# Operand sums in tiles of their own, and one unit of the second output pair ahead of the first pair's last

## The chip, the cores and the metric

The kernel runs on one core of a Trainium2 chip. The metric is the device time of one execution in microseconds (us); the time of a kernel is the median of several executions.

## The reference, cut to what matters

The program computes two layers of a transformer trunk on 512 tokens of width 1024: a token mixer (differential attention in the first layer, gated linear attention in the second) beside a cross-attention, and then a gated MLP with a causal convolution of width 3. The change lies in the MLP:

```python
def conv_ffn(h, w_up, conv_w, conv_b, w_down):
    u = h @ w_up                       # 1024 -> 2 * 2816
    c = conv(u, conv_w) + conv_b       # depthwise, width 3, causal
    a, g = jnp.split(c, 2, axis=-1)
    return (jax.nn.silu(g) * a) @ w_down
...
h = rms_norm(x, ffn_norm[i])
x = x + conv_ffn(h, w_up[i], conv_w[i], conv_b[i], w_down[i])
```

All of it is float32.

## The kernel before, in words

**Layout.** Activations lie transposed: a tile holds 128 channels (partitions) by 512 tokens. Each float32 operand of a matmul is split into two parts, `hi` (a rounded copy, made by ScalarE) and `lo` (operand minus `hi`, made by VectorE), and a product is three matmuls: hi x hi, hi x lo, lo x hi. Weights come from HBM in blocks of 128 x 1024 through three `raw` tiles (loads on SyncE's queue, line 266) and are split into `whi` and `wlo` tiles, six of each (`WB`, lines 257 and 260, or 308 to 312).

**The MLP in parts.** `ffn` (from line 1168) runs once for each layer. The 2816 hidden channels are 11 units of 256 channels (`q`), taken in three parts of 4, 4 and 3 units (`HALVES`). A unit is four up products: for each of its two tiles of 128 channels (`n`) one product for `a` ("ua") and one for the gate ("ug"). Each product is scaled and convolved by `conv` (lines 1248 to 1252: VectorE, ScalarE, VectorE, VectorE) into a `cvo` tile; then come SiLU on ScalarE (line 1446) and the multiplication on VectorE (line 1448). So there are four convolutions in a unit, of which the third and the fourth belong to its second tile. Some "ua" products (`SEVEN`) are done by seven products on sums instead.

**The down projection by seven products.** At the end of a part, `down` (from line 1339) multiplies the hidden channels by the down weights and adds the result to the residual. It takes 2 x 2 blocks: two tiles of channels, two tiles of output channels, and two halves of the tokens, and uses seven block products instead of eight, with sums of the operands. `seven(c, m)` (line 1352) is one unit of that: output pair `c` (0 to 3), hidden unit `m`. It has seven steps of three matmuls, 21 in all, each 128 x 128 by 256 columns (line 1359). `own` is its first three steps, which need only split halves of the hidden tiles themselves, and `mixed` is its other four, which need the sums. The list `seq` (lines 1402 to 1404) gives the order of the units by hand. When a unit is the last that uses a weight block, `release` lets a next block be made. A pair's last unit is followed by `decode` (line 1367), which adds the four banks to the residual. The last part of the first layer does without the seven products.

**The sums of the hidden operands.** When both tiles of a unit are there, `mid_sums` (line 1298) calls `combine` (line 1281), four subtractions of 256 columns (line 1287). For the last unit of a part VectorE makes them, in two `cvo` tiles of 512 columns. For the others POOL makes them, in one `wsum` tile of 1024 columns, and their split into `hi` and `lo` (`parts_of`, lines 1278 and 1279) is put off: it is kept in `later` and issued by `behind` (line 1313) behind the third convolution that follows. `wsum` has two buffers. They also hold the sums of the weight blocks, which POOL makes (`block_sums`, line 285; cast and subtraction at lines 311 and 312), and the sums of token tiles (`token_sums`, line 1325). `cvo` has six buffers.

**What sets the order.** TensorE runs in the order in which the program is written. On VectorE, ScalarE and SyncE a planner of the framework sets the order at build time: by when its own estimates say that an instruction's inputs and buffers are ready, earlier written ones first. POOL's sums keep their written order. At run time every engine takes its instructions strictly in the order so set.

Of the kernel before, what the change touches and what calls it, by code (L numbers as in the profile page):

```python
# [11 lines left out]
F32 = mybir.dt.float32  # L12
# [9 lines left out]
S = 512  # L22
# [162 lines left out]
def trunk(ctx, tc, head_d, x_t, mem_t, wpack, cols_a_d, cols_d, conv_d, gate_d, rel_bias, diff_lambda, consts, onehot, out):  # L185
    nc = tc.nc
    mm = nc.tensor.matmul
    V, A, G = nc.vector, nc.scalar, nc.gpsimd
# [23 lines left out]
    def blk(b, w=128):  # L212
        return slice(w * b, w * b + w)
# [40 lines left out]
    at = [0]  # L254
# [70 lines left out]
    def sum_tile():  # L325
        return sum_pool[0].tile([128, WTILE], F32, name="wsum", bufs=2)
# [172 lines left out]
    E = mybir.EngineType  # L499
    load = nc.sync.dma_start  # L500
    with tc.tile_pool(name="ini", bufs=1) as ip, tc.manual_schedule(engines={E.Activation, E.DVE, E.Pool, E.SP}):
# [34 lines left out]
        parts, acc, split_w = [], [None], [None]  # L536
# [631 lines left out]
    def ffn(pool, l, acc):  # L1168
# [37 lines left out]
            refill()  # L1206

        def ctile():
            return pool.tile([128, S], F32, name="cvo", bufs=6)

        def up(i, n):
            p, = take(1)
# [34 lines left out]
        def conv(p, j):  # L1247
            V.tensor_mul(p, p, rB)
            c = ctile()
            first = A.activation(c, p, AF.Identity, scale=cv[l][:, 2, j:j + 1], bias=cv[l][:, 3, j:j + 1])  # L1250
            V.scalar_tensor_tensor(c[:, 1:], p[:, :S - 1], cv[l][:, 1, j:j + 1], c[:, 1:], op0=ALU.mult, op1=ALU.add)
            final = V.scalar_tensor_tensor(c[:, 2:], p[:, :S - 2], cv[l][:, 0, j:j + 1], c[:, 2:], op0=ALU.mult, op1=ALU.add)
            if later:
                convs[0] += 1
                if convs[0] == 3:
                    convs[0] = 0
                    behind(first, final)
            return c
# [19 lines left out]
            A.copy(hi, t)  # L1278
            V.tensor_sub(lo, t, hi.bitcast(F32))  # L1279

        def combine(b2, b1, bh, bl, fh, fl, E, parts):
            t = [ctile(), ctile()] if E is V else [sum_tile()]
            q = [blk(i, 256) for i in range(4)]
            at = lambda i: t[i // 2][:, q[i % 2]] if E is V else t[0][:, q[i]]
            for i, x, y in ((0, b1[:, right], b1[:, left]), (1, b2[:, right], at(0)), (2, b2[:, right], b1[:, right]),
                            (3, b2[:, left], at(1))):
                ins = E.tensor_sub(at(i), x, y)  # L1287
                if E is G:
                    tc.keep_in_program_order(ins)
            parts(t)  # L1290
            return q
# [6 lines left out]
        def mid_sums(c2, ops, E):  # L1298
            h, lo = (pool.tile([128, 2 * S], F32R, name="mid2", bufs=8) for _ in range(2))

            def parts(t):
                for i, x in enumerate(t):
                    c = blk(i, 2 * S // len(t))
                    if E is V:
                        parts_of(x, h[:, c], lo[:, c])
                    else:
                        later.append((x, h[:, c], lo[:, c]))
            q = combine(*c2, *ops, E, parts)
            return operands([h[:, c] for c in q], [lo[:, c] for c in q], *ops)

        later, convs = [], [0]
# [8 lines left out]
        def scaled(k):  # L1320
            t = ctile()
            A.activation(t, xT[k], AF.Copy, scale=c_ffn(l, k))
            return t

        def token_sums(ks):
            (bh, bl), (fh, fl) = (tokens[k] for k in ks)
            tiles = [split_tiles(pool, "vs", 12) for _ in range(2)]

            def parts(t):
                for i, (hi, lo) in enumerate(tiles):  # L1330
                    parts_of(t[0][:, blk(i, S)], hi, lo)
            combine(scaled(ks[0]), scaled(ks[1]), None, None, None, None, G, parts)
            h, lo = ([t[i][:, c] for t in tiles for c in (left, right)] for i in range(2))
            sums_of[ks] = operands(h, lo, bh, bl, fh[:, left], fl[:, left])

        place = [(2, left), (0, left), (0, right), (1, left), (1, right), (2, right), (3, left)]
        steps, close = (1, 2, 0, 5, 4, 6, 3), {2: 0, 5: 2, 6: 3, 3: 1}

        def down(base, nq, mids, pairs, last, acc2):
            first = used[0]  # L1340
            whole = [plan[first + c][0][0] == "dw" for c in range(4)]
            banks, seen = {}, [set() for _ in range(4)]

            def start(c):
                begin(("dw" if whole[c] else "dn", l, base, c))
                banks[c] = take(2 if whole[c] else 4)

            def emitted(c, m):
                if m == nq - 1 or m % 2:
                    release(first + c, 1 if whole[c] else 2, m == nq - 1)  # L1350

            def seven(c, m, some=steps):
                while len(made) <= first + c or len(made[first + c]) <= m:
                    refill()
                for i in some:
                    b, h = place[i]
                    (hi, lo), (bh, bl) = made[first + c][m][i], mids[m][i]
                    for t, (w, v) in enumerate(((hi, bh), (hi, bl), (lo, bh))):
                        mm(banks[c][b][:, h], w, v, start=b not in seen[c], stop=m == nq - 1 and t == 2 and i in close)  # L1359
                        seen[c].add(b)  # L1360
                if some[-1] != steps[-1]:
                    return
                emitted(c, m)
                if m == nq - 1:
                    decode(c)

            def decode(c):
                b, x1, x2, u, y = banks[c], xT[2 * c], xT[2 * c + 1], ctile(), ctile()[:, left]
                A.copy(u[:, left], b[2][:, left])
                V.tensor_add(x1, x1, b[0])  # L1370
                V.tensor_add(y, u[:, left], b[2][:, right])
                V.tensor_add(u[:, right], y, b[1][:, right])
                V.tensor_add(y, y, b[3][:, left])
                V.tensor_add(x2, x2, b[1])
                V.tensor_add(x1, x1, u)
                x2v = x2.rearrange("p (h c) -> p h c", h=2)
                V.tensor_add(x2v, x2v, y.unsqueeze(1).to_broadcast([128, 2, 256]))
                if last and l == 1:
                    for n in (2 * c, 2 * c + 1):
                        nc.sync.dma_start(out[n], xT[n])  # L1380

            def eight(c, n, m0, m1, total=nq):
                parts = whole_piece(first + c)
                product(banks[c][n], parts, n, pairs, range(2 * m0, 2 * m1), 2 * total)

            if all(whole):
                for c0 in (0, 2):
                    cs = (c0, c0 + 1)
                    for c in cs:
                        start(c)  # L1390
                        for n in range(2):
                            eight(c, n, 0, nq - 1)
                        emitted(c, 1)
                    for c in cs:
                        for n in range(2):
                            eight(c, n, nq - 1, nq)
                            update(2 * c + n, banks[c][n], lambda k: c_attn(1, k), acc2)
                            nc.sync.dma_start(xres[2 * c + n], xT[2 * c + n])
                        emitted(c, nq - 1)
                return  # L1400
            own, mixed = steps[:3], steps[3:]
            seq = [(0, m, steps) for m in range(nq - 1)] + [(1, 0, steps), (0, nq - 1, own), (1, 1, own), (0, nq - 1, mixed)]
            seq += [(1, 1, mixed)] + [(1, m, steps) for m in range(2, nq)]
            seq += [(c, m, steps) for c in ((2,) if whole[3] else (2, 3)) for m in range(nq)]
            for c, m, some in seq:
                if c not in banks:
                    start(c)
                seven(c, m, some)
            if whole[3]:
                start(3)  # L1410
                eight(3, 0, 0, nq)
                V.tensor_add(xT[6], xT[6], banks[3][0])
                nc.sync.dma_start(out[6], xT[6])
                eight(3, 1, 0, nq - 1, nq - 1)
                V.tensor_add(xT[7], xT[7], banks[3][1])
                for t, p, queue in zip((left, right), take(2), (nc.sync, nc.scalar)):
                    p = p[:, :S // 2]
                    parts = made[first + 3]
                    product(p, parts[-2:], 1, [(bh[:, t], bl[:, t]) for bh, bl in pairs[-2:]])
                    V.tensor_add(xT[7][:, t], xT[7][:, t], p)  # L1420
                    queue.dma_start(out[7, :, t], xT[7][:, t])

        base, acc2 = 0, None
        for part, nq in enumerate(HALVES):
            mids, pairs = [], []
            last = part == len(HALVES) - 1
            for q in range(base, base + nq):
                c2, ops, at, cs = [], [], {}, {}
# [11 lines left out]
                for n in range(2):  # L1440
# [13 lines left out]
                    else:  # L1454
                        m = mid_tile()
# [104 lines left out]
```

## Time and profile before

| what | us |
|---|---|
| median of 3 runs (1152.59 to 1152.91) | 1152.81 |
| the profiled execution | 1153.93 |
| its span, first to last instruction | 1152.0 |
| TensorE busy in the span | 1141.9 |
| VectorE busy | 931.4 |
| ScalarE busy | 616.4 |
| POOL busy | 270.1 |

The profile is of one execution. PE is TensorE's matmul queue, PEld its weight loads, DVE VectorE, ACT ScalarE, POOL GpSimd, SP SyncE. A row of a timeline has the start in us from the beginning of the span, the duration in us, the engine, the line of the kernel, the operation, the tiles written and read (`out<-in`), their shapes, a count of merged instructions, and in brackets how long the engine was idle before it and what ended that. Ends of matmuls are modelled by the profiler, so waits of TensorE are better taken from the starts of its matmuls. A row of the waits has total us, times and longest us. The rows of a tile or line have the shortest, middle and longest duration in ns.

### The profile page before, as it was taken

How to read it: one execution, taken by the hardware profiler on the slowest of the kernel's cores; microseconds unless marked ns; L12 is line 12 of the kernel's file. 1: busy time of each engine (PE TensorE's matmuls, PEld its weight loads, DVE VectorE, ACT ScalarE, POOL GpSimd, SP SyncE). 2: the span in 40 equal slices, each digit the busy share in tenths (PEclk: the TensorE clock that was granted, in tenths of full speed). 3: DMA queues.
4: the chain of work that ended last, by engine and by line, in shares of the span. 5: the costliest groups of instructions: out<-in, count | busy, mean ns of one | idle time of the engine just before them, and what ended most of it. 6: DMA issues, size and time to landing. Idle time of an engine off the chain costs nothing.

```text
span 1152.0 us, 17410 instructions
## 1 busy us (share of the span) xinstructions
PE 1141.9 (99%) x6527; PEld 993.4 (86%) x6527; DVE 931.4 (81%) x1531; ACT 616.4 (54%) x1080; POOL 270.1 (23%) x318
## 2 busy tenths in 40 slices
PE   9999999999999999999999999999999999999998
PEld 7888888888889888898888888988888989899888
DVE  7676778688889789999677637777898988999987
ACT  6676686556554454445457634535664434544552
POOL 0000000003364423740000000000245432476241
PEclk9999999999999999999999999999999999999999
DMA  8522242133314332344252220333232343224312
GB/s 286 175 82 87 78 142 74 57 109 92 110 56 146 93 92 73 93 128 126 71 176 73 94 97 16 92 126 126 73 92 74 95 126 104 89 76 137 105 51 101
DMA packets 39666, 117.86 MB, mean 102 GB/s; under 512 B 4768, under 2 KB 7257, under 8 KB 39583
## 3 DMA queue, kind: packets, MB, share of 16 engines
q1 hardware_dynamic: 39150, 116.37, 32.0%
q8 instruction: 51, 0.84, 0.3%
q10 hardware_dynamic: 432, 0.39, 0.1%
q14 instruction: 33, 0.26, 0.1%
HBM read 112.54 MB, written 4.21 MB: 101 GB/s over the span
## 4 chain that ended last, share of the span: by engine, by line
PE 80%; DVE 13%; ACT 4%; issue 2%; POOL 1%; ACTq 0%; POOLq 0%; DVEq 0%
PE ps_mm L385 6%; PE ps_mm L408 6%; PE ps_mm L407 6%; PE ps_mm L409 6%; PE ps_mm L387 6%; PE ps_mm L386 6%; PE ps_lg L1359 3%; PE ps_sm L408 3%; PE ps_sm L407 3%; PE ps_sm L409 3%; PE ps_mm L1359 3%; PE ps_tp L224 3%; PE ps_lg L1233 3%; PE ps_tp L1359 2%; PE ps_sm L1359 2%; DVE mid L1279 2%
## 5 line engine op out<-in xcount | busy, mean ns | idle before, releaser
L260 DVE TENSOR_TENSOR wlo<-raw,whi 128x1024 fp32r<-128x1024 f32 (+5 forms) x166 | 188.7, 1148 | 74.7 <-ACT whi L257 73.8
L257 ACT CAST whi<-raw 128x1024 fp32r<-128x1024 f32 (+5 forms) x166 | 157.9, 967 | 104.9 <-PE ps_mm L408 24.3
L385 PE MATMUL ps_mm<-whi,xsh 128*128 128x512 f32 (+2 forms) x328 | 126.3, 385 | 0.0
L387 PE MATMUL ps_mm<-whi,xsl 128*128 128x512 f32 (+2 forms) x328 | 123.0, 375 | 0.0
L386 PE MATMUL ps_mm<-wlo,xsh 128*128 128x512 f32 (+2 forms) x328 | 122.8, 374 | 0.0
L407 PE MATMUL ps_mm<-xsh,whi 128*128 128x512 f32 x310 | 121.8, 393 | 0.0
L408 PE MATMUL ps_mm<-xsl,whi 128*128 128x512 f32 x310 | 120.9, 390 | 0.0
L409 PE MATMUL ps_mm<-xsh,wlo 128*128 128x512 f32 x310 | 120.8, 390 | 0.0
L285 POOL TENSOR_TENSOR wsum<-raw 128x256 f32<-128x256 f32 (+1 forms) x108 | 87.8, 834 | 117.5 <-DMA raw<-in_wpack_dram 64.1
L1287 POOL TENSOR_TENSOR wsum<-cvo 128x256 f32<-128x256 f32 x40 | 33.9, 848 | 226.7 <-DVE cvo L1448 140.9
L407 PE MATMUL ps_sm<-xsh,whi 128*128 128x512 f32 x202 | 78.6, 389 | 0.0
L408 PE MATMUL ps_sm<-xsl,whi 128*128 128x512 f32 x202 | 78.6, 389 | 0.0
L409 PE MATMUL ps_sm<-xsh,wlo 128*128 128x512 f32 x202 | 78.6, 389 | 0.0
L312 DVE TENSOR_TENSOR wlo<-wsum,whi 128x1024 fp32r<-128x1024 f32 (+1 forms) x54 | 70.6, 1307 | 8.9 <-ACT whi L311 8.9
L311 ACT CAST whi<-wsum 128x1024 fp32r<-128x1024 f32 (+1 forms) x54 | 51.9, 962 | 39.8 <-POOL wsum L285 39.5
L385 PEld LDWEIGHTS ps_mm<-whi,xsh 128*128 128x128 f32 x328 | 61.7, 188 | 11.4 <-issue 1.0
L387 PEld LDWEIGHTS ps_mm<-whi,xsl 128*128 128x128 f32 x328 | 61.7, 188 | 11.3
L386 PEld LDWEIGHTS ps_mm<-wlo,xsh 128*128 128x128 f32 x328 | 61.8, 188 | 10.1
L409 PEld LDWEIGHTS ps_mm<-xsh,wlo 128*128 128x128 f32 x310 | 58.2, 188 | 12.1
L407 PEld LDWEIGHTS ps_mm<-xsh,whi 128*128 128x128 f32 x310 | 58.2, 188 | 11.9 <-issue 0.3
L408 PEld LDWEIGHTS ps_mm<-xsl,whi 128*128 128x128 f32 x310 | 58.3, 188 | 11.9 <-DVE xsl L366 0.4
L1263 POOL MEMSET xsh<- 128x128 f32 x2 | 0.4, 210 | 277.5 <-PE ps_sm L408 191.0
(428 smaller groups left out, 3144.9 us busy)
## 6 DMA issues: line engine op xcount, KB each, us to landing
raw<-in_wpack_dram SPq DMA_DIRECT2D x178, 512.0 KB, 3.6
xt<-in_x_t_dram SPq DMA_DIRECT2D x15, 256.0 KB, 5.2
raw<-in_wpack_dram SPq DMA_DIRECT2D x15, 256.0 KB, 2.8
raw<-in_wpack_dram SPq DMA_DIRECT2D x8, 384.0 KB, 3.3
xres<-xt SPq DMA_DIRECT2D x8, 256.0 KB, 3.4
xt<-xres SPq DMA_DIRECT2D x8, 256.0 KB, 5.7
out_dram<-xt SPq DMA_DIRECT2D x7, 256.0 KB, 2.0
bt<-bias_d SPq DMA_DIRECT2D x6, 256.0 KB, 4.3
```

The costliest lines, as they stand in the source:

```text
L257: ins = A.copy(hi[:, c], raw[:, c])
L260: V.tensor_sub(lo[:, c], raw[:, c], hi[:, c].bitcast(F32))
L285: tc.keep_in_program_order(getattr(G, "tensor_" + op)(o, x, y))
L311: A.copy(h1[:, m], wsum[:, m])
L312: V.tensor_sub(l1[:, m], wsum[:, m], h1[:, m].bitcast(F32))
L385: mm(p, sh[k][:, blk(b)], hi, start=k == 0, stop=False)
L386: mm(p, sh[k][:, blk(b)], lo, start=False, stop=False)
L387: mm(p, sl[k][:, blk(b)], hi, start=False, stop=k == KT - 1)
L407: mm(p, hi[:, blk(n)], bh, start=i == first, stop=False)
L408: mm(p, hi[:, blk(n)], bl, start=False, stop=False)
L409: mm(p, lo[:, blk(n)], bh, start=False, stop=i == last)
L1359: mm(banks[c][b][:, h], w, v, start=b not in seen[c], stop=m == nq - 1 and t == 2 and i in close)
```

## The change

The mid sums of every unit, POOL's too, go into two `cvo` tiles; `cvo` gets a seventh buffer, and the DMA scratch in SBUF is halved. `wsum` keeps its two buffers, for weight blocks and token sums. The put-off split, now two pieces of 512 columns instead of one of 1024, is issued behind the second convolution that follows instead of the third. In the parts of four units, unit (1,1) is done whole ahead of unit (0,3): the order was (0,0) (0,1) (0,2) (1,0), own steps of (0,3), own steps of (1,1), mixed steps of (0,3), mixed steps of (1,1), (1,2) (1,3), and it becomes (0,0) (0,1) (0,2) (1,0) (1,1) (0,3) (1,2) (1,3). The part of three units keeps its order.

```diff
         def ctile():
-            return pool.tile([128, S], F32, name="cvo", bufs=6)
+            return pool.tile([128, S], F32, name="cvo", bufs=7)
...
                 convs[0] += 1
-                if convs[0] == 3:
+                if convs[0] == (2):
                     convs[0] = 0
                     behind(first, final)
...
-        def combine(b2, b1, bh, bl, fh, fl, E, parts):
-            t = [ctile(), ctile()] if E is V else [sum_tile()]
+        def combine(b2, b1, E, t, parts):
             q = [blk(i, 256) for i in range(4)]
-            at = lambda i: t[i // 2][:, q[i % 2]] if E is V else t[0][:, q[i]]
+            at = lambda i: t[i // 2][:, q[i % 2]] if len(t) > 1 else t[0][:, q[i]]
...
-            q = combine(*c2, *ops, E, parts)
+            q = combine(*c2, E, [ctile(), ctile()], parts)
...
-            combine(scaled(ks[0]), scaled(ks[1]), None, None, None, None, G, parts)
+            combine(scaled(ks[0]), scaled(ks[1]), G, [sum_tile()], parts)
...
             own, mixed = steps[:3], steps[3:]
-            seq = [(0, m, steps) for m in range(nq - 1)] + [(1, 0, steps), (0, nq - 1, own), (1, 1, own), (0, nq - 1, mixed)]
-            seq += [(1, 1, mixed)] + [(1, m, steps) for m in range(2, nq)]
+            seq = [(0, m, steps) for m in range(nq - 1)] + [(1, 0, steps)]
+            if nq > 3:
+                seq += [(1, 1, steps), (0, nq - 1, steps)] + [(1, m, steps) for m in range(2, nq)]
+            else:
+                seq += [(0, nq - 1, own), (1, 1, own), (0, nq - 1, mixed), (1, 1, mixed), (1, 2, steps)]
...
-    nc = _bacc.Bacc("TRN2", target_bir_lowering=False, num_devices=1, dynamic_dma_scratch_size=512)
+    nc = _bacc.Bacc("TRN2", target_bir_lowering=False, num_devices=1, dynamic_dma_scratch_size=256)
```

## The prediction, made before the changed kernel ran

> **What bounds the kernel now.** I read the page first, then who waited for whom on TensorE, then the order of time on each engine around those waits.
>
> ```profile
> span 1152.0 us, 17410 instructions
> ...
> PE 1141.9 (99%) x6527; PEld 993.4 (86%) x6527; DVE 931.4 (81%) x1531; ACT 616.4 (54%) x1080; POOL 270.1 (23%) x318
> ```
>
> TensorE is busy 1141.9 of 1152.0 us, and the change neither adds nor removes a matmul. So only what TensorE loses to waiting can be won, some 10 us in the whole kernel. The view of the waits on TensorE says which:
>
> ```profile
> PE ps_tp L1359 <- DVE mid L1279: 3.2, 4, 1.3
> PE ps_sm L1359 <- DVE mid L1279: 2.7, 4, 0.8
> ```
>
> Columns: total us, times, longest. Both rows are the seven-product matmuls of the down projection (line 1359), held up by VectorE's low half of the mid operands (line 1279). All eight waits lie in the four stages with `nq` = 4. I call them A (layer 0, first part), B (layer 0, second part), C and D (the same of layer 1). Stage B on TensorE in order of time:
>
> ```profile
> 456.30 0.40 PE L1359 MATMUL ps_lg<-mid,whi 128*128 128x256 f32 x2
> ...
> 458.82 0.40 PE L1359 MATMUL ps_lg<-mid,whi 128*128 128x256 f32 x2
> ...
> 470.81 0.39 PE L1359 MATMUL ps_tp<-mid,whi 128*128 128x256 f32 x1 [0.44 <-DVE mid L1279]
> ...
> 472.55 0.38 PE L1359 MATMUL ps_tp<-mid,whi 128*128 128x256 f32 x1 [0.76 <-DVE mid L1279]
> ...
> 474.68 0.40 PE L1359 MATMUL ps_mm<-mid,whi 128*128 128x256 f32 x2
> ```
>
> First column: start. The first unit runs from 456.30 to 458.82, so a unit of 21 matmuls takes 2.52 us, a matmul 0.12 and a step of three 0.36. The seventh unit of the list, (1,2), starts at 474.68; six units after 456.30 it would be 456.30 + 15.12 = 471.42. Stage B loses **3.26 us**. Its last release (472.55) comes 2.13 before the seventh unit. The other three stages, start and last release:
>
> ```profile
> 328.68 0.28 PE L1359 MATMUL ps_mm<-mid,whi 128*128 128x256 f32 x1
> ...
> 343.06 0.39 PE L1359 MATMUL ps_sm<-mid,whi 128*128 128x256 f32 x1 [0.76 <-DVE mid L1279]
> ```
>
> ```profile
> 882.80 0.28 PE L1359 MATMUL ps_mm<-mid,whi 128*128 128x256 f32 x1
> ...
> 898.49 0.39 PE L1359 MATMUL ps_sm<-mid,whi 128*128 128x256 f32 x1 [0.76 <-DVE mid L1279]
> ```
>
> ```profile
> 1011.74 0.28 PE L1359 MATMUL ps_lg<-mid,whi 128*128 128x256 f32 x1
> ...
> 1025.87 0.39 PE L1359 MATMUL ps_tp<-mid,whi 128*128 128x256 f32 x1 [0.76 <-DVE mid L1279]
> ```
>
> Loss = last release + 2.13 - start - 15.12: A 1.39, C 2.70, D 1.14. With B's 3.26 the four stages lose **8.49 us**. That is all this change can win there.
>
> Why is VectorE late? Stage B on VectorE, behind the third convolution of the last unit:
>
> ```profile
> 458.32 1.75 DVE L1279 TENSOR_TENSOR mid<-wsum,mid 128x1024 fp32r<-128x1024 f32 x1
> 460.00 0.69 DVE L1248 TENSOR_TENSOR ps_sm<-ps_sm,rB 128x512 f32<-128x512 f32 x1
> 461.79 1.37 DVE L312 TENSOR_TENSOR wlo<-wsum,whi 128x1024 fp32r<-128x1024 f32 x1 [1.10 <-ACT whi L311]
> ...
> 465.36 1.16 DVE L1448 TENSOR_TENSOR cvo<-cvo 128x512 f32<-128x512 f32 x1 [0.76 <-ACT cvo L1446]
> 466.56 1.72 DVE L1287 TENSOR_TENSOR cvo<-cvo 128x256 f32<-128x256 f32 x2
> ...
> 469.74 0.41 DVE L1287 TENSOR_TENSOR cvo<-cvo 128x256 f32<-128x256 f32 x1
> 470.07 0.68 DVE L1279 TENSOR_TENSOR mid<-cvo,mid 128x512 fp32r<-128x512 f32 x1
> 470.68 1.22 DVE L312 TENSOR_TENSOR wlo<-wsum,whi 128x1024 fp32r<-128x1024 f32 x1
> 471.81 0.68 DVE L1279 TENSOR_TENSOR mid<-cvo,mid 128x512 fp32r<-128x512 f32 x1
> ```
>
> The fourth convolution (460.00) had its product at about 456.3, when TensorE turned to the down projection. VectorE got to it 3.7 us late, directly behind the 1.75 us split of the previous unit's sums. Then it stood for 1.10 on ScalarE's cast at line 311. That cast waited for POOL, and POOL for a `wsum` buffer:
>
> ```profile
> 460.71 1.05 ACT L311 CAST whi<-wsum 128x1024 fp32r<-128x1024 f32 x1 [3.55 <-POOL wsum L285]
> 456.14 1.44 POOL L285 TENSOR_TENSOR wsum<-raw 128x256 f32<-128x256 f32 x2 [3.49 <-DVE wlo L312]
> ```
>
> POOL stood 3.49 us until line 312 freed one of the two `wsum` buffers; the other held the mid sums that wait for their split. So one tile kind causes both delays.
>
> **The change part by part.**
>
> *Order of the units.* Unit (1,1) goes whole before (0,3). It moves 21 matmuls and, with them, the release of a weight block. That release lets one block of pair 2 be made: two casts on ScalarE, two subtractions on VectorE, four on POOL, one load from SyncE, all of them once as before, but now possibly ahead of the last mid tile. (0,3) now starts at start + 12.60 and not 10.08. Its sums come in two tiles: the first must be there after the three own steps and one matmul, at start + 12.60 + 1.08 + 0.12 = 13.80, the second two steps later, at 14.52. With VectorE exactly as now, the second tile (the releases above) against the second: A 343.06 for 343.20, in time; B 472.55 for 470.82, 1.73 late; C 898.49 for 897.32, 1.17 late; D 1025.87 for 1026.26, in time. Lost 2.90 instead of 8.49: the order alone gives **5.6 us**. What is late next: the weights of (1,2), in B the line 312 row that ends at 471.90, needed at 471.42 plus two matmuls, 471.66. It is covered as soon as VectorE runs 0.24 earlier, and until then it lies behind the 1.73. The decode of pair 0 follows (0,3), which now ends at start + 15.12 = 471.42 in B; today its last two steps lie behind the release at 472.55, so the decode is not later than it is.
>
> What the release can cost: it comes at start + 12.60, in B 468.90, and a cast goes first. Only in B does the second tile start later than that with VectorE as early as I work out below (471.81 - 1.5 = 470.3). Its bounds are nothing and two subtractions of at most 1.22, 2.4 us. I take nothing, since the mid tiles are issued earlier and today's rows put the blocks in gaps of the chain; the other end gives 1147.0 and lies in the range.
>
> *Sums in `cvo` tiles.* Fourteen units put their sums into two tiles of 512 and not one of 1024. Prices, min/median/max in ns:
>
> ```profile
> L1279 DVE TENSOR_TENSOR mid<-cvo,mid x54: 407/683/991, 266.1 to 1127.3; 128x512 fp32r<-128x512 f32 x38, 128x256 fp32r<-128x256 f32 x16
> L1279 DVE TENSOR_TENSOR mid<-wsum,mid x14: 1208/1222/1758, 289.9 to 1115.5; 128x1024 fp32r<-128x1024 f32 x14
> L1287 POOL TENSOR_TENSOR wsum<-cvo x40: 729/741/1727, 268.4 to 1105.4; 128x256 f32<-128x256 f32 x40
> L1448 DVE TENSOR_TENSOR cvo<-cvo x44: 676/693/1293, 264.2 to 1122.5; 128x512 f32<-128x512 f32 x44
> ```
>
> Two halves cost 2 x 0.683 = 1.37 against 1.22 undisturbed: 14 x 0.15 = 2 us more VectorE work in all, hidden by TensorE except ahead of the four stages, where I count it. POOL's four subtractions stay as they are. POOL gets its second `wsum` back, so the wait of 3.49 and with it VectorE's 1.10 should go.
>
> *Split behind the second convolution.* The 1.75 goes from directly ahead of the fourth convolution; 1.37 comes in one convolution earlier. VectorE is nearly gapless there, so I take the difference only, 0.38, and not the whole 1.75. With the 1.10 VectorE is earlier by 1.48; I take **1.5**. Bounds: with the split in idle time and both collisions with POOL gone (1.16 against 0.69, 1.72 against 2 x 0.41) 1.75 + 1.10 + 0.47 + 0.90 = 4.2 earlier; on the other side the rival below.
>
> *Seventh `cvo` buffer, half the DMA scratch.* Space only: the kernel issues its DMAs from SyncE and ScalarE, none from POOL, and their number and sizes stay. I cost it at nothing from both sides.
>
> *Sum.* With VectorE 1.5 earlier, A, C and D lose nothing and B 1.73 - 1.5 = 0.23. Won: 8.49 - 0.23 = 8.26 us. The profiled execution took 1153.93 for its span of 1152.0, 1.12 above the median of 1152.81; the stalls are differences inside one span, so I take them off the median: **1144.6 us**.
>
> **The rivals.**
>
> *The planner does not do it* (VectorE as now). The order on VectorE and ScalarE is a planner's, by its own estimates. If the split lands where it was and the cast at line 311 is still queued ahead of the fourth convolution, only the order of units works: 1152.81 - 5.6 = 1147.2. For: the line 311 cast also needs a weight buffer that the last up product frees. Against: the 3.49 wait names `wsum`.
>
> *POOL moves into the chain.* POOL's block sums start up to 3.5 us sooner and meet other two-input operations of VectorE. A collision costs up to 1.293 - 0.693 = 0.60; three new ones are 1.8, VectorE is then 0.3 later than now. Lost: A 0.16, B 2.03, C 1.47, D 0: 3.7, won 4.8, 1148.0. Against: the same POOL work only shifts, and the rows at 465.36 and 466.56 already pay for it. [...]
>
> *`cvo` runs short, slower than before.* Pending sums now hold two of seven buffers where the rest had six, so five are left. A convolution of the next unit that finds none waits for POOL's four subtractions, 4 x 0.741 = 2.96, with every later VectorE step of that unit behind it. If VectorE is x later than now in all four stages, the loss is 2.90 + 4x - 0.14 - 0.39; it reaches 8.49 at x = 1.5. From there on the change is slower; at x = 2.96 the loss is 14.2, **1158.5**. For: nothing in this trace shows how full the six are. Against: the split comes one convolution earlier, so the two buffers are back before the unit's second half asks for its tiles.
>
> *It cancels out.* x between 1.0 and 2.0 by the same sum, lost 6.4 to 10.4, within 2.2 us of today.
>
> **How the numbers follow.** Forecast 0.55 (1143.5 to 1146), planner 0.13, POOL 0.10 (both 1146 to 1150.5), cancelling 0.08, `cvo` 0.14. A difference under 0.2%, 2.3 us, is about what a measurement of this kernel can't tell from no change. Faster is 0.55 + 0.13 + 0.10 = 0.78, same 0.08, slower 0.14. The low end is all 8.49 gone plus some tenths from elsewhere: 1143.5. The high end takes in both partial cases and the edge of cancelling: 1150.5.
>
> **What would show it.** Right: no wait of line 1359 on line 1279 in the four stages beyond 0.3 us; the mid split ahead of the third convolution's operations; POOL's line 285 no longer waiting 3.5 us for line 312 ahead of stage B; stage starts 2.52 x 6 ahead of their seventh unit. Wrong: waits of line 1250 for POOL or for a `cvo` buffer; a new wait of line 1359 on line 312 or on a PSUM bank; TensorE busy sums that differ outside the four stages.

## The result, and the profile after

The changed kernel takes **1150.8 us** (median of 20 runs, 1150.19 to 1152.8); the kernel before, on the same chips, 1152.87 (20 runs, 1151.86 to 1154.33). The ratio is 0.9984, with a 95% interval of 0.9977 to 0.9990: 2.1 us won where 8.3 were forecast, and 0.3 us above the range. In the changed kernel most lines of the MLP stand one lower: the seven-product matmuls are line 1358, the decode lines 1368 to 1376, the sums line 1286.

The page's first rows:

```profile
span 1149.3 us, 17442 instructions
...
PE 1141.0 (99%) x6527; PEld 993.1 (86%) x6527; DVE 928.9 (81%) x1545; ACT 617.1 (54%) x1094; POOL 273.9 (24%) x318
```

The waits on TensorE (total us, times, longest):

```profile
PE ps_tp L1358 <- DVE cvo L1370: 2.5, 2, 1.7
PE ps_sm L1358 <- DVE cvo L1370: 1.5, 2, 1.1
```

The eight waits on the mid split are gone, all of them. Four new ones stand in their place, one in each stage, and they are on line 1370: the second addition of `decode(0)`, which reads PSUM bank 2 of pair 0. Pair 2 gets that bank, and the third step of its first unit, (2,0), is the first to write it. TensorE around it, in time:

```profile
328.75 0.40 PE L1358 MATMUL ps_mm<-mid,whi 128*128 128x256 f32 x2
...
350.12 0.47 PE L1358 MATMUL ps_sm<-mid,whi 128*128 128x256 f32 x2 [0.34 <-DVE cvo L1370]
...
455.87 0.40 PE L1358 MATMUL ps_lg<-mid,whi 128*128 128x256 f32 x2
...
477.73 0.48 PE L1358 MATMUL ps_tp<-mid,whi 128*128 128x256 f32 x2 [0.83 <-DVE cvo L1370]
...
880.42 0.40 PE L1358 MATMUL ps_mm<-mid,whi 128*128 128x256 f32 x2
...
902.60 0.47 PE L1358 MATMUL ps_sm<-mid,whi 128*128 128x256 f32 x2 [1.14 <-DVE cvo L1370]
...
1008.34 0.40 PE L1358 MATMUL ps_lg<-mid,whi 128*128 128x256 f32 x2
...
1031.05 0.47 PE L1358 MATMUL ps_tp<-mid,whi 128*128 128x256 f32 x2 [1.68 <-DVE cvo L1370]
```

Eight units and two steps after a stage's first matmul make 8 x 2.52 + 0.72 = 20.88 us. The third step of (2,0) is late against that by 0.49, 0.98, 1.30 and 1.83 in A to D, 4.60 in all. About 0.4 more follows in each stage, most of it at the fifth step, which needs the next bank of the decode. From the starts of all matmuls a stage loses A 0.89, B 1.37, C 1.69, D 2.23, together **6.18 us**. So 8.49 was won at the seventh unit, 0.37 in the second layer's part of three units, and 6.18 was given back: 2.68, and the spans differ by 1152.0 - 1149.3 = 2.7.

Why the decode is late: VectorE, stage A, after the change.

```profile
340.53 1.21 DVE L312 TENSOR_TENSOR wlo<-wsum,whi 128x1024 fp32r<-128x1024 f32 x1
...
343.35 0.67 DVE L1369 TENSOR_TENSOR xt<-xt,ps_mm 128x512 f32<-128x512 f32 x1
343.94 1.21 DVE L312 TENSOR_TENSOR wlo<-wsum,whi 128x1024 fp32r<-128x1024 f32 x1
345.08 1.49 DVE L309 TENSOR_TENSOR wlo<-raw,whi 128x768 fp32r<-128x768 f32 x1
348.28 1.36 DVE L312 TENSOR_TENSOR wlo<-wsum,whi 128x1024 fp32r<-128x1024 f32 x1 [1.71 <-ACT whi L311]
349.57 0.41 DVE L1370 TENSOR_TENSOR cvo<-cvo,ps_sm 128x256 f32<-128x256 f32 x1
```

Before, the decode's second addition stood directly behind its first:

```profile
342.93 0.68 DVE L1370 TENSOR_TENSOR xt<-xt,ps_mm 128x512 f32<-128x512 f32 x1
343.52 0.41 DVE L1371 TENSOR_TENSOR cvo<-cvo,ps_sm 128x256 f32<-128x256 f32 x1
```

Now three weight splits stand between the two, and the last one, at 348.28, waits. ScalarE and POOL say for what:

```profile
347.20 1.05 ACT L311 CAST whi<-wsum 128x1024 fp32r<-128x1024 f32 x1 [2.78 <-POOL wsum L285]
```

```profile
341.87 2.15 POOL L285 TENSOR_TENSOR wsum<-raw 128x256 f32<-128x256 f32 x2 [4.96 <-issue]
343.99 1.77 POOL L285 TENSOR_TENSOR wsum<-wsum,raw 128x256 f32<-128x256 f32 x1
345.83 1.33 POOL L285 TENSOR_TENSOR wsum<-raw,wsum 128x256 f32<-128x256 f32 x1
```

The last split belongs to the second weight block of pair 2, which unit (2,2) needs at about 328.75 + 10 x 2.52 = 353.95. Its sums are made by POOL until 347.16. POOL began them only at 341.87, just after VectorE's split of 340.53 had ended (341.74) and with that a `wsum` buffer was free; the view names no releaser for these 4.96 us, and the run with a third `wsum` buffer below tests the reading. So an operation wanted 4 us later holds up one that TensorE wants at once: VectorE stands idle for 1.71 us ahead of the split and still does not take line 1370, which is queued behind it.

How it came to stand there can be read in the code. `seven` writes a unit's matmuls, then `emitted` (the release, by which a block is made), then `decode`. Before, the first block of pair 2 was written at the end of (0,3), ahead of `decode(0)`, and the second at the end of (1,1), behind it. With (1,1) written ahead of (0,3), both blocks are written ahead of `decode(0)`, and the planner sets earlier written work first.

### The profile page after: what moved, and what is told of

Its sections match the earlier page's. It is cut to its first block, busy times and chain, and to the rows that moved or that the text cites. A ratio compares the mean times of both kernels' runs of the same rounds, so it can differ in the third digit from the quotient of the medians.

```text
span 1149.3 us, 17442 instructions
## 1 busy us (share of the span) xinstructions
PE 1141.0 (99%) x6527; PEld 993.1 (86%) x6527; DVE 928.9 (81%) x1545; ACT 617.1 (54%) x1094; POOL 273.9 (24%) x318
## 4 chain that ended last, share of the span: by engine, by line
PE 96%; POOL 1%; DVE 1%; ACT 1%; issue 0%; POOLq 0%; ACTq 0%
PE ps_mm L407 7%; PE ps_mm L408 7%; PE ps_mm L409 7%; PE ps_mm L385 6%; PE ps_mm L387 6%; PE ps_mm L386 6%; PE ps_sm L409 4%; PE ps_sm L408 4%; PE ps_sm L407 4%; PE ps_lg L1358 4%; PE ps_mm L1358 3%; PE ps_tp L1358 3%; PE ps_tp L408 3%; PE ps_tp L407 3%; PE ps_tp L409 3%; PE ps_tp L224 3%
## 5 line engine op out<-in xcount | busy, mean ns | idle before, releaser
L285 POOL TENSOR_TENSOR wsum<-raw 128x256 f32<-128x256 f32 (+1 forms) x108 | 98.2, 930 | 118.4 <-DMA raw<-in_wpack_dram 44.8
L1286 POOL TENSOR_TENSOR cvo<-cvo 128x256 f32<-128x256 f32 x56 | 47.4, 866 | 135.9 <-DVE cvo L1450 134.8
L312 DVE TENSOR_TENSOR wlo<-wsum,whi 128x1024 fp32r<-128x1024 f32 (+1 forms) x54 | 66.8, 1237 | 15.2 <-ACT whi L311 15.1
```

The lines of the kernel that those rows point to most:

```text
L285: tc.keep_in_program_order(getattr(G, "tensor_" + op)(o, x, y))
L312: V.tensor_sub(l1[:, m], wsum[:, m], h1[:, m].bitcast(F32))
```

## The experiments

| kernel | median us (runs) | before, same chip | ratio, interval |
|---|---|---|---|
| order alone | 1158.34 (5) | 1152.65 | 1.0045, 1.0032 to 1.0058 |
| tiles and early split, old order | 1144.51 (5) | 1152.65 | 0.9931, 0.9918 to 0.9943 |
| change, decode written first | 1145.75 (5) | 1152.65 | 0.9942, 0.9928 to 0.9955 |
| change, release of (1,1) held | 1144.62 (5) | 1152.65 | 0.9932, 0.9919 to 0.9944 |
| early split alone | 1144.88 (5) | 1153.06 | 0.9929, 0.9917 to 0.9942 |
| tiles alone, split where it was | 1154.42 (11) | 1153.06 | 1.0012, 1.0003 to 1.0021 |
| order alone, decode written first | 1148.08 (5) | 1153.06 | 0.9960, 0.9947 to 0.9972 |
| change, 3 wsum, 5 cvo | 1156.99 (7) | 1153.06 | 1.0031, 1.0020 to 1.0042 |
| change, 5 cvo | 1163.45 (5) | 1152.89 | 1.0092, 1.0078 to 1.0106 |
| tiles and early split, old order, 6 cvo | 1144.89 (5) | 1152.89 | 0.9931, 0.9917 to 0.9945 |

My theory: the new order puts pair 2's second block ahead of `decode(0)` on VectorE, and that costs what the new waits show. Rivals: the split tiles or the seventh buffer cost it, POOL's sums meeting VectorE cost it, or the order gains less than I worked out.

**The order alone**, on the kernel before:

```diff
-            seq = [(0, m, steps) for m in range(nq - 1)] + [(1, 0, steps), (0, nq - 1, own), (1, 1, own), (0, nq - 1, mixed)]
-            seq += [(1, 1, mixed)] + [(1, m, steps) for m in range(2, nq)]
+            seq = [(0, m, steps) for m in range(nq - 1)] + [(1, 0, steps)]
+            if nq > 3:
+                seq += [(1, 1, steps), (0, nq - 1, steps)] + [(1, m, steps) for m in range(2, nq)]
+            else:
+                seq += [(0, nq - 1, own), (1, 1, own), (0, nq - 1, mixed), (1, 1, mixed), (1, 2, steps)]
```

> The kernel before with only the new order of units ((1,1) whole ahead of (0,3)). Theory W (a weight block that is written ahead of the decode holds the decode up on VectorE, and TensorE then waits for pair 0's bank): the mid waits fall from 8.5 to about 3 us, but 5 to 7 us come back at the start of pair 2, time 1152 to 1155 us, no gain. My prediction's step (the order alone gives 5.6 and the decode is no later than before): 1147.2. Rival T (the loss comes with the sums in cvo tiles): also about 1147.

It took 1158.34 us, more than the 1152 to 1155 expected. The waits on TensorE:

```profile
PE ps_sm L1359 <- DVE cvo L1371: 3.6, 2, 1.8
PE ps_tp L1359 <- DVE cvo L1371: 3.4, 2, 1.8
```

Line 1371 is here the decode's second addition. The new waits come with the order, without the tiles and without the seventh buffer. The stages lose 3.84, 3.89, 3.72 and 2.14, 13.6 in all, where before lost 8.49. In A and B nearly 3 us of it are a slower clock (last section), which the expectation didn't count.

**The tiles and the early split, with the old order**: the change with `seq` of before (the two lines with a minus above).

> The changed kernel with the old order of units. Theory W: pair 0 is decoded as in the kernel before, with no wait at pair 2; the mid waits shrink because VectorE is 1 to 4 us earlier, to about 2 us of 8.5; time about 1146 us. Rival T: the waits at pair 2 stay, about 1150.5 us.

1144.51 us, below the 1146 expected: no mid waits are left at all. TensorE waits in none of the stages, and the span is 1142.7. This half of the change brings the whole 8.1 us; the new order takes about 6 of it back.

**The change with the decode written first**:

```diff
                 if some[-1] != steps[-1]:
                     return
-                emitted(c, m)
                 if m == nq - 1:
                     decode(c)
+                emitted(c, m)
```

> The changed kernel with decode(c) written ahead of the release of the pair's last weight block, two lines swapped. Theory W: the waits at pair 2 (6.2 us in four stages) go, time 1144 to 1145.5 us. Rival L (the decode is late because unit (0,3) itself ends later, whatever is written ahead): 1150 to 1151 us.

1145.75 us, 0.25 above the range expected. VectorE in stage A:

```profile
343.41 0.67 DVE L1369 TENSOR_TENSOR xt<-xt,ps_mm 128x512 f32<-128x512 f32 x1
344.01 1.21 DVE L312 TENSOR_TENSOR wlo<-wsum,whi 128x1024 fp32r<-128x1024 f32 x1
345.14 0.41 DVE L1370 TENSOR_TENSOR cvo<-cvo,ps_sm 128x256 f32<-128x256 f32 x1
...
349.56 1.76 DVE L312 TENSOR_TENSOR wlo<-wsum,whi 128x1024 fp32r<-128x1024 f32 x1
```

The line 312 split that stood ahead of line 1370 now stands behind the whole decode, and nobody waits for it. One split (344.01) still stands between the two additions and costs TensorE nothing. The four new waits are gone. The part of three units of the second layer loses 0.37 here, which the next run doesn't.

**The change with the release of (1,1) held** until (0,3) and its decode are written:

```diff
                 if some[-1] != steps[-1]:
                     return
+                if nq == 4 and (c, m) == (1, 1):
+                    return
                 emitted(c, m)
                 if m == nq - 1:
                     decode(c)
+                if nq == 4 and (c, m) == (0, 3):
+                    emitted(1, 1)
```

> The changed kernel, with the release that follows unit (1,1) held until unit (0,3) is decoded; the units keep their new order. Theory W: pair 2's first block then follows (0,3), its second the decode, as in the kernel before; the waits at pair 2 go, 1144 to 1145.5 us. If the early first block is what costs and not the second, this one gains and the swap of decode and release does not. Rival L: 1150 to 1151 us.

1144.62 us, no wait in the stages. Matmuls, tiles and buffers are those of the change; only the place of one block's making differs. With the run before it, this shows the cause.

**The early split alone**, on the kernel before (`wsum` sums, six `cvo`, old order):

```diff
-                if convs[0] == 3:
+                if convs[0] == 2:
```

> The kernel before with one digit changed: the put-off split is issued behind the second convolution instead of the third; sums stay in wsum, order of units and buffers as before. Theory S (the place of the split makes VectorE early): mid operands 1.5 to 3 us earlier, mid waits 8.5 to under 2 us, time 1144.5 to 1147 us. Theory P (the wsum buffer that POOL waits for makes it): the splits still share wsum, VectorE gains at most the 0.4 us of the split itself, time 1150 to 1152 us.

1144.88 us: one digit brings all that the changed tiles and the digit bring together. VectorE in stage B, whose first down matmul is here at 454.95:

```profile
447.45 1.61 DVE L1279 TENSOR_TENSOR mid<-wsum,mid 128x1024 fp32r<-128x1024 f32 x1
...
456.62 0.68 DVE L1248 TENSOR_TENSOR ps_sm<-ps_sm,rB 128x512 f32<-128x512 f32 x1
457.21 1.21 DVE L312 TENSOR_TENSOR wlo<-wsum,whi 128x1024 fp32r<-128x1024 f32 x1
458.35 0.74 DVE L1251 SCALAR_TENSOR_TENSOR cvo<-ps_sm,cv,cvo 128x511 f32<-128x511 f32 x1
...
465.35 1.28 DVE L1279 TENSOR_TENSOR mid<-cvo,mid 128x512 fp32r<-128x512 f32 x2
466.55 1.21 DVE L312 TENSOR_TENSOR wlo<-wsum,whi 128x1024 fp32r<-128x1024 f32 x1
```

Measured from the stage's start, the fourth convolution begins at 1.67, before at 460.00 - 456.30 = 3.70: 2.03 earlier. The split of line 312 behind it no longer stands still and takes 1.21, before 1.10 and 1.37: some 1.3 more. And the last two mid splits follow each other (x2), with the weight split behind them and not between: the rest, 1.1. The last mid operand is ready at 11.68, before at 16.19.

**The tiles alone**, split behind the third convolution as before, old order, seven `cvo`:

> Sums in cvo tiles with the seventh buffer, old order of units, the split still behind the third convolution. Theory P: POOL has both wsum buffers, VectorE is 1 to 1.5 us earlier, time 1147 to 1149 us. Theory S: 1150.5 to 1152.5 us, as the kernel before.

1154.42 us. Waits on TensorE and, below them, of POOL:

```profile
PE ps_tp L1358 <- DVE mid L1279: 2.8, 4, 1.1
PE ps_tp L1358 <- ACT mid L1278: 1.9, 2, 1.0
PE ps_sm L1358 <- DVE mid L1279: 1.4, 4, 0.6
```

```profile
POOL wsum L285 <- DVE wlo L312: 52.5, 20, 12.0
```

The mid sums no longer lie in `wsum`, and still POOL waits for a `wsum` buffer, 52.5 us in 20 waits; before it was 32.6 in 15. The mid operands are as late as before on the whole: in A and B to 0.1 us, in C 1.7 earlier, in D 2.0 later. The time is even 1.4 us above before, beyond the ranges of both theories; theory S, no gain without the early split, is the nearer one. A buffer comes free when VectorE has done its split, so more room doesn't help where VectorE is what is late.

**The order alone, with the decode written first**, on the kernel before: the edits of the first and the third experiment.

> The kernel before with the new order of units, and the decode written ahead of the release. It tests my step 'the order alone gives 5.6' with the decode taken out of it. Theory W: mid waits as in the run of the order alone (1.6 us at the seventh unit), no wait at pair 2, time 1145 to 1147.5 us. Rival L: the waits at pair 2 stay, 1152 us or more.

1148.08 us, 5.0 less than before, where my step had 5.6 for the order, and 0.6 above the range expected here. There is no wait at pair 2. The seventh unit still waits in two stages, 0.29 in B and 1.34 in C, and the part of three units of the second layer loses 1.26, before 0.37.

**The change with a third wsum buffer**, and `cvo` cut to five to make room:

```diff
-        return sum_pool[0].tile([128, WTILE], F32, name="wsum", bufs=2)
+        return sum_pool[0].tile([128, WTILE], F32, name="wsum", bufs=3)
...
-            return pool.tile([128, S], F32, name="cvo", bufs=7)
+            return pool.tile([128, S], F32, name="cvo", bufs=5)
```

> The changed kernel with a third wsum buffer, paid for with two cvo buffers (seven to five). VectorE's order around the decode is the changed kernel's. Theory W2 (the decode is late because a weight split ahead of it waits for POOL's sums, and these wait for wsum): the sums of pair 2's second block start 4 us sooner, the decode comes 2 to 4 us sooner, waits at pair 2 fall from 6.2 to under 1.5, time 1144.5 to 1146.5 us. If three splits ahead of the decode are enough by themselves: 1150 to 1151.5 us. If five cvo buffers are too few: above 1151.5, with waits of the convolutions.

1156.99 us. It has to be read against a control: **the change with five cvo and two wsum**.

> The changed kernel with five cvo buffers in place of seven and two wsum buffers as in the change: the control of the run with a third wsum buffer, which took 1157.0 us with two waits of the seventh matmul unit on the mid split. Two theories. One: the third wsum buffer lets GpSimd fill sums in the stretch of the last splits, where VectorE's operations then take longer (1.76 in place of 1.21 us for the 128x1024 split); then five cvo buffers alone cost nothing, the time is that of the change, 1150 to 1152 us, and the waits are again the four on the decode of 0.9 to 2.2 us. The other: five cvo buffers are too few, the scaling of a convolution waits for GpSimd's sum that still reads one; then this kernel too takes 1155 to 1159 us, and the seventh unit waits on the mid split.

1163.45 us, more than either theory gave. The waits on TensorE with five `cvo` and two `wsum`:

```profile
PE ps_tp L1358 <- DVE cvo L1370: 5.7, 2, 2.9
PE ps_sm L1358 <- DVE cvo L1370: 4.1, 2, 2.9
```

With five `cvo` and three `wsum`:

```profile
PE ps_tp L1358 <- DVE mid L1279: 4.6, 5, 1.4
PE ps_sm L1358 <- DVE mid L1279: 1.6, 2, 1.1
```

With the third `wsum` buffer no wait on line 1370 is left. Stage A shows it by itself, since TensorE loses nothing there: POOL makes the sums in question from 336.29 on, 7.55 us after the stage's start and in the change 13.12, no split stands idle ahead of line 1370, and that line starts at 19.90, in the change at 20.82. The three splits still stand ahead of it, and the 0.9 us are less than the 2 to 4 expected, but they are enough. In B to D TensorE itself is later by then, so these say less. So the decode did wait through `wsum`. But the mid splits are 1.6 to 2.1 us later in each of the four stages than in the control. VectorE in stage B, same instructions in the same order, first with three `wsum`, then with two:

```profile
456.65 1.76 DVE L312 TENSOR_TENSOR wlo<-wsum,whi 128x1024 fp32r<-128x1024 f32 x1
...
466.30 2.61 DVE L1286 TENSOR_TENSOR cvo<-cvo 128x256 f32<-128x256 f32 x3
```

```profile
458.68 1.21 DVE L312 TENSOR_TENSOR wlo<-wsum,whi 128x1024 fp32r<-128x1024 f32 x1
...
467.25 1.51 DVE L1286 TENSOR_TENSOR cvo<-cvo 128x256 f32<-128x256 f32 x3
```

1.76 for 1.21 and 2.61 for 1.51. In the first kernel POOL works beside them; in the second it stands idle until 460.02, while the split runs (a row of each):

```profile
456.09 2.92 POOL L285 TENSOR_TENSOR wsum<-raw 128x256 f32<-128x256 f32 x2
```

```profile
460.02 2.16 POOL L285 TENSOR_TENSOR wsum<-raw 128x256 f32<-128x256 f32 x2 [1.87 <-ACT whi L308]
```

The control also shows what five `cvo` cost by themselves. VectorE ahead of its stage B:

```profile
428.38 0.42 DVE L1239 TENSOR_TENSOR cvo<-cvo,ps_lg 128x256 f32<-128x256 f32 x1 [2.02 <-POOL cvo L1286]
```

The addition after an up product waits 2.02 us for POOL's subtractions to give a tile back, ahead of B, of D and of the second layer's part of three units (6.1 us in all); ahead of C a convolution's activation waits as long. The last mid operand of B is ready 14.59 us after the stage's start, in the change 12.19, and the decode is later by as much. That the wait of 2.02 makes the 2.40 is likely, but wasn't followed step by step. Part of both kernels' time is a slower clock: 0.997 with three `wsum` and 0.995 with two, the means of the profiled executions (last section).

**Six cvo instead of seven**, with tiles, early split and old order, and the DMA scratch of the kernel before:

> The change with the old order of the units and six cvo buffers, as before the change, in place of seven. If the seventh buffer is what keeps the separate operand tiles from a shortage, as the rival of short cvo buffers had it, some convolution's activation waits for a sum and the time rises from 1144.5 us towards the rival's 1158.5; by my theory the split place carries the gain and the tiles need nothing: 1144 to 1146 us, with no wait of the seventh unit.

1144.89 us, no wait in the stages. With the old order the seventh buffer isn't needed, and the halved DMA scratch, which the run with seven had, costs nothing that shows. Whether six are enough with the new order wasn't tried.

No kernel beats the 1144.5 to 1144.9 of four of these; their ranges touch, and TensorE loses nothing to the seven products in them.

## Why the prediction was wrong, step by step

*What bounds the kernel, and what can be won.* Right: the 8.49 us at the seventh unit could be won and were won. Four kernels without stage losses stand 8.0 to 8.2 us below before; the fifth, the change with the decode written first, stands 6.9 below, and the 0.37 that it loses in the last part explain about a third of the difference; the rest stays open.

*The step that failed: "so the decode is not later than it is".* I compared TensorE's times only: (0,3) ends where its last release had been. But the decode runs on VectorE, and its time is also set by what is queued ahead of it there. Line 1370 starts 20.82 us after stage A's start (349.57 - 328.75), before 14.84 (343.52 - 328.68). I did count that the moved release (the release behind (1,1)) lets a block be made, with two casts and two subtractions, but asked only whether these come ahead of the mid tiles (bounds nothing to 2.4 us). They came behind the mid tiles and ahead of the decode. I didn't follow the second consumer of the order I had moved: pair 2, which waits for pair 0's bank. The list of signs named "a new wait of line 1359 on line 312 or on a PSUM bank"; no rival had a price for it. Measured: 6.2 us in the change.

*The order alone gives 5.6.* Right in size for what it counted: 5.0 with the decode written first, where the four stages lose 1.63 in place of 8.49 and the last part 0.9 more. As the change writes it, it loses 5.7 by itself, nearly 3 of that through the clock, and on top of the early split about 6.

*The split's place, 0.38, and wsum, 1.10: x = 1.5.* Too small, and put down to the wrong edit. In the change VectorE's last mid operand is earlier, from the stage's start, by 2.48, 4.00, 3.13 and 1.03 in A to D, mean 2.66. The early split alone does this (2.41, 4.52, 3.37 and 2.42), and without any change to `wsum`; the tiles without the early split gain nothing. "I take the difference only" was the mistake. The 1.75 us split did not merely change its price and move: in the run with the early split alone, stage B, with it gone from directly ahead of the fourth convolution, the convolution came forward by 2.03, the cast and sum chain of line 312 lost its wait, and the planner put a weight split behind the last mid split instead of between the two. With x that large the old order already loses nothing, so the new order had nothing left to bring.

*The planner does not do it.* It did: the mid operands came earlier in all four stages.

*POOL moves into the chain.* Not in the change: the mid operands were earlier in every stage. With a third `wsum` buffer it happened, 1.6 to 2.1 us per stage against the 1.8 the rival was priced at. The row of 1.76 for 1.21 has its like in the kernel before: of the 44 multiplications of line 1448, the 34 that no POOL operation overlapped took 0.68 to 0.70 us, the ten beside which POOL worked 1.15 to 1.29.

*cvo runs short.* Not with seven, nor with six and the old order. The view of the change does name the sign that I had listed, line 1250 waiting for POOL:

```profile
ACT cvo L1250 <- POOL wsum L285: 7.2, 3, 2.6
```

But line 285 makes weight sums and uses no `cvo` tile, and each time VectorE's scaling, the convolution's own input, ended within 0.05 us of it (the first: activation at 431.15, scaling ended at 431.03, POOL's hidden sums at 427.32). So the input set the time. With five buffers the shortage comes, 2.0 us at each of four places.

*It cancels out.* The time came out near this case by luck, through a mechanism it didn't have.

## What to carry to other kernels

Where engines run strictly in order, as VectorE did here (idle for 1.71 us with line 1370 queued behind), moving a step on one engine moves everything it issues in the queues of the others: list what then stands ahead of each consumer, the one that frees a PSUM bank above all. Write what frees a shared resource ahead of work that is only preparation, and look at the longest instruction directly ahead of a late chain first: here one digit that moved it was worth 8 us. Try the parts of a change one by one, since one part can eat what another wins.

## What the runs showed of the hardware that was not expected

**About 2 us of standing still can be followed by half TensorE's clock.** In the kernel with the order alone, stage A, TensorE stood until 350.88:

```profile
350.88 0.47 PE L1359 MATMUL ps_sm<-mid,whi 128*128 128x256 f32 x2 [1.79 <-DVE cvo L1371]
...
352.50 0.41 PE L1359 MATMUL ps_mm<-mid,wlo 128*128 128x256 f32 x1
352.71 0.63 PE L1359 MATMUL ps_sm<-mid,whi 128*128 128x256 f32 x2
353.14 0.41 PE L1359 MATMUL ps_sm<-mid,wlo 128*128 128x256 f32 x1
```

The same kernel by windows (from and to, length, TensorE busy, granted clock, DMA share, GB/s):

```profile
349.00:351.90 2.90, 1.04 (x7) 1.00 0.62 172
351.90:355.30 3.40, 3.36 (x16) 0.50 0.00 0
355.30:358.70 3.40, 3.40 (x30) 1.00 0.45 154
```

For 3.4 us the clock is 0.50 (in the trace from 351.908 to 355.321, 3.413 us), and a step of three matmuls takes 0.64 (352.50 to 353.14) and not 0.36. Stage A loses 3.84 us, where the stall (350.88 - 348.81 - 0.12 = 1.95, from the start of the matmul before it) and the 0.39 that follows in every stage make 2.34: 1.5 us are the clock's.

The same follows in stage B, from 481.61, and in three stages of the control with five `cvo`, whose stalls are 3.0 (granted clock 0.98 on the mean of 75 to 80 us around each of B, C and D, 1.00 around A). It also follows in C and D of the kernel with three `wsum` and five `cvo`, from 897.50 and 1027.21, and there TensorE stood twice, 0.65 and 1.35, with a few matmuls between. C and D lose 4.01 each in that kernel, and B, with the same two stalls at full clock, 2.47: about 3 us of its time are the clock's and not POOL's.

Length alone doesn't decide: the change's own longest stall, 1.83 in D, had no such sequel, nor had one of 2.01 in stage C of the kernel with the order alone, as long as the one in its stage B. The place in time may, but no run tested it. The half-clock stretches of that kernel begin 129.70 us apart (481.61 - 351.91), 38.0 times the 3.413 us that one lasts. An estimate from these two starts: counted on from 351.91 in steps of 129.70 / 38 us, the stalls of A (348.93 to 350.88) and B (479.31 to 481.32) lie whole in the step just ahead of the half clock, while the edge of a step, at 908.3, cuts stage C's stall (907.41 to 909.42) in two. Where the border lies stays open too: in stage B of the kernel before, stalls of 1.45 and 0.60 close together (up to 468.67 and 470.81) had no sequel.

So a stall of 1.95 us had a second price in stage A: 1.5 us.
